# MLP down projections of a two-layer trunk: 24 rows by seven products and 8 plain rows, against all 32 rows by seven products

## Chip, cores and metric

The kernel runs on one core of one Trainium2 chip. The metric is device time in microseconds (us) for one execution of the whole program: both layers, from the input rows to the output rows.

## What is computed

The program is the forward pass of a trunk of two layers over 1024 tokens of width 1024. The part that matters here is the squared-ReLU MLP of each layer, the residual that follows it, and what reads that residual. From the reference, cut:

```python
def squared_relu_mlp(h, w_up, w_down):          # w_up 1024 x 4096, w_down 4096 x 1024
    return jnp.square(jax.nn.relu(h @ w_up)) @ w_down
...
    h = modulate(rmsnorm(x, norm_g[l, 2]), sh_f, sc_f)
    y = squared_relu_mlp(h, mlp_up_w[l], mlp_down_w[l])
    x = x + g_f[:, None, :] * rmsnorm(y, norm_g[l, 3])
```

After layer 0 the next reader of `x` is the attention mixer of layer 1 (`modulate(rmsnorm(x, ...))` times `q_a_w`, and the keys and values). After layer 1 `x` is the output.

## The kernel before

**Numbers.** Each float32 operand is split into a high and a low part (`split_w`, L163 on ACT for the high part, L164 on DVE for the low part), and one product is three matmuls (`mm`, L160): low by high, high by low, high by high. A matmul takes a 128x128 stationary tile and 512 moving columns.

**Seven products.** A down projection is, for a pair of the 128-deep blocks of the 4096 hidden features, a 2 by 2 block product: tokens in two halves of 512, output columns in two halves of 512. `mlp_up` makes the hidden activations, and `sums` (L1052) forms from them seven combined operands, kept in DRAM as `ha0` to `ha6`, one 128x512 tile per pair and operand. `down_pairs` runs through the seven products (Winograd's form of Strassen's seven) as seven **stages**: one operand `ha[which]` against one block of the weights ("11", "12", "21", "22") or a difference of blocks. A stage has its steps over `i`; a step holds two pairs, so four blocks of 128 rows. For each step SP loads a 512 KB operand tile (`raw<-ha`), ACT and DVE split it into a `ring` tile `pa`, the weight block is split into a ring tile `pb`, and PE does 24 matmuls: four token tiles of 128, two blocks, three matmuls. Four PSUM banks (named `one`, or `mm` and `tp`) collect the four token tiles, and at the end of a stage `copy`, `add` or `sums` brings them into the rows `y` (eight tiles of 128 tokens by 1024).

**What the seven products cover.** In the kernel before `ROWS = 8` of the 32 blocks are left out of the pairs: their hidden activations go to DRAM whole (`hd`), and `PAIRS` is 12, six steps per stage. After the seven stages those eight rows are multiplied plainly in `down` (`fill_row` loads and splits a row's weights and activations, 48 matmuls for each of eight token tiles and each group of rows: 384 in all for eight rows, counted in `big<-slot`). The groups are 2, 2 and 4 rows; in the last group each token tile becomes complete in turn.

**The seam.** As a token tile becomes complete, `Seam.tile` adds it to `y` (L300), takes the sum of squares on ACT (L249) and the root (L251, L256), multiplies by the root and the gate on DVE (L306), adds the residual row from DRAM (`xs`, L307), stores the new row and, in layer 0, norms it again for the next layer (`flush`, L289). `Seam.load` brings the residual rows through the same four buffers (`raw_tile`) that all loads use. In layer 0 the normed rows are transposed on PE (L402), scaled and shifted on ACT (L404) and split, and `first_block` multiplies them by the first three column blocks of `q_a_w`, whose three 512 KB loads use the same four buffers. `latent` then takes the norm of those latents; its matmul with `ones` (L1129) is the first that needs a finished latent.

**What sets the order.** The program is written in plain loops, and a scheduler sets the order on each engine from it. `pinned` ties the instructions written inside it to the order in which they are written, on the engines named (all but SP without an argument). Each engine works through its own queue in order. SP issues the loads.

## Time and profile before

| | before |
|---|---|
| runs | 2185.59, 2186.09 and 2193.38 us, median 2186.09 us |
| profiled execution | span 2186.4 us, 0.3 us above the median of the runs |
| instructions | 25316 |
| PE, DVE, ACT busy | 2101.2, 1523.9 and 1052.9 us |
| stages of the program (us from the start) | conv to 397, MLP up of layer 0 to 716, pair stages to 956, plain rows to 1055, latents and attention to 1540, MLP up of layer 1 to 1856, pair stages to 2090, plain rows to 2186.4 |

The profile gives the busy time of each engine, the chain of waits that ended last, groups of equal instructions with their mean time and what ended the idle time ahead of them, and the time of the loads from issue to landing. PE is TensorE's matmuls, DVE is VectorE, ACT is ScalarE, SP issues the loads. Both down projections are short against the whole, so a row must be taken from its stage: the two MLP down projections are the stretches from 716 to 1055 and from 1856 to the end.

### The profile page before, as it was taken

How to read it: one execution, taken by the hardware profiler on the slowest of the kernel's cores; microseconds unless marked ns; L12 is line 12 of the kernel's file. 1: busy time of each engine (PE TensorE's matmuls, PEld its weight loads, DVE VectorE, ACT ScalarE, POOL GpSimd, SP SyncE). 2: the span in 40 equal slices, each digit the busy share in tenths (PEclk: the TensorE clock that was granted, in tenths of full speed). 3: DMA queues.
4: the chain of work that ended last, by engine and by line, in shares of the span. 5: the costliest groups of instructions: out<-in, count | busy, mean ns of one | idle time of the engine just before them, and what ended most of it. 6: DMA issues, size and time to landing. Idle time of an engine off the chain costs nothing.

```text
span 2186.4 us, 25316 instructions
## 1 busy us (share of the span) xinstructions
PE 2101.2 (96%) x9702; PEld 1728.0 (79%) x9702; DVE 1523.9 (70%) x2001; ACT 1052.9 (48%) x1501; POOL 4.0 (0%) x8
## 2 busy tenths in 40 slices
PE   4999999899999999999899999999899999999998
PEld 3778888678888788888777888878688887888886
DVE  6777766876565679776788776665865655566665
ACT  4533354744454444344665555564645444444422
POOL 0000000000000000000000000000000000000000
PEclk9999999999999999999999999999999999999999
DMA  7435464256443985554224231053254544853343
GB/s 226 132 119 152 130 205 139 78 166 194 155 159 117 339 291 189 167 170 143 77 63 125 68 112 44 30 171 128 66 171 155 179 165 149 301 174 97 123 137 116
DMA packets 233551, 323.61 MB, mean 148 GB/s; under 512 B 18165, under 2 KB 141394, under 8 KB 233430
## 3 DMA queue, kind: packets, MB, share of 16 engines
q1 hardware_dynamic: 198424, 244.11, 35.8%
q10 hardware_dynamic: 35006, 77.89, 9.4%
q8 instruction: 76, 1.25, 0.3%
q14 instruction: 45, 0.37, 0.1%
HBM read 244.35 MB, written 77.59 MB: 147 GB/s over the span
## 4 chain that ended last, share of the span: by engine, by line
PE 78%; DVE 12%; ACT 6%; DMA 2%; issue 2%; ACTq 0%; SPq 0%; DVEq 0%
PE one L160 39%; PE mm L160 19%; PE big L160 9%; PE tp L160 6%; ACT junk L249 2%; PE big L1285 2%; DVE y L306 2%; DVE raw L307 2%; PE tp L1311 1%; DVE y L300 1%; DVE acc L190 1%; DVE small L1288 1%; DMA raw<-in_ada_w_dram 1%; DMA aw<-in_ada_w_dram 1%; ACT small L251 1%
## 5 line engine op out<-in xcount | busy, mean ns | idle before, releaser
L160 PE MATMUL one<-slot,uphi 128*128 128x512 f32 x1224 | 378.3, 390 | 0.0
L160 PE MATMUL big<-slot 128*128 128x512 f32 x1536 | 353.0, 390 | 0.5 <-DVE slot L164 0.4
L160 PEld LDWEIGHTS big<-slot 128*128 128x128 f32 x1536 | 287.7, 188 | 60.0 <-DVE slot L164 0.9
L160 PEld LDWEIGHTS one<-slot,uphi 128*128 128x128 f32 x1224 | 230.7, 188 | 48.4 <-issue 0.5
L160 PE MATMUL one<-slot,uplo 128*128 128x512 f32 x612 | 240.9, 394 | 8.1 <-ACT y L568 2.3
L164 DVE TENSOR_TENSOR uplo<-raw,uphi 128x1024 fp32r<-128x1024 f32 x127 | 153.1, 1221 | 133.9 <-ACT uphi L163 133.8
L160 PE MATMUL one<-ring,ring 128*128 128x512 f32 x864 | 197.9, 390 | 3.6 <-DVE ring L164 3.6
L163 ACT ACTIVATE ring<-w 128x1024 fp32r<-128x1024 f32 x84 | 88.9, 1059 | 225.6 <-PE tp L160 117.6
L163 ACT ACTIVATE uphi<-raw 128x1024 fp32r<-128x1024 f32 x127 | 134.5, 1061 | 121.6 <-PE one L160 89.1
L160 PEld LDWEIGHTS one<-ring,ring 128*128 128x128 f32 x864 | 161.7, 188 | 38.7 <-ACT ring L163 3.1
L160 PE MATMUL mm<-slot,uphi 128*128 128x512 f32 x520 | 166.6, 401 | 9.5 <-DVE slot L367 9.3
L164 DVE TENSOR_TENSOR ring<-w,ring 128x1024 fp32r<-128x1024 f32 x84 | 102.7, 1222 | 87.9 <-ACT ring L163 86.1
L160 PEld LDWEIGHTS one<-slot,uplo 128*128 128x128 f32 x612 | 115.5, 189 | 35.4 <-ACT y L493 3.3
L160 PE MATMUL mm<-ring,ring 128*128 128x512 f32 x576 | 139.5, 390 | 0.0
L160 PE MATMUL tp<-ring,ring 128*128 128x512 f32 x576 | 138.7, 389 | 0.0
L190 DVE SCALAR_TENSOR_TENSOR acc<-raw,csil,acc 128x1024 f32<-128x1024 f32 x88 | 112.8, 1282 | 32.3 <-DMA raw<-in_ada_w_dram 30.0
L160 PEld LDWEIGHTS mm<-ring,ring 128*128 128x128 f32 x576 | 107.6, 188 | 23.5 <-issue 0.8
L160 PEld LDWEIGHTS tp<-ring,ring 128*128 128x128 f32 x576 | 108.1, 188 | 22.4
L160 PEld LDWEIGHTS mm<-slot,uphi 128*128 128x128 f32 x520 | 98.9, 192 | 32.8 <-DVE slot L367 10.8
L493 ACT ACTIVATE y<-one 128x512 f32<-128x512 f32 x66 | 39.0, 591 | 163.4 <-PE one L160 102.2
L160 PE MATMUL one<-slot,s 128*128 128x512 f32 x468 | 112.6, 389 | 0.0
L164 DVE TENSOR_TENSOR ring<-raw,ring 128x1024 fp32r<-128x1024 f32 x84 | 102.4, 1219 | 11.8 <-ACT ring L163 11.8
(255 smaller groups left out, 3515.8 us busy)
## 6 DMA issues: line engine op xcount, KB each, us to landing
ha<-y ACTq DMA_DIRECT2D x168, 256.0 KB, 4.2
raw<-ha SPq DMA_DIRECT2D x84, 512.0 KB, 4.1
raw<-in_ada_w_dram SPq DMA_DIRECT2D x80, 512.0 KB, 3.9
raw<-in_mlp_up_w_dram SPq DMA_DIRECT2D x70, 512.0 KB, 4.2
w<-in_mlp_down_w_dram SPq DMA_DIRECT2D x48, 512.0 KB, 6.3
raw<-hd SPq DMA_DIRECT2D x32, 512.0 KB, 4.4
hd<-y ACTq DMA_DIRECT2D x24, 512.0 KB, 3.7
xs<-raw ACTq DMA_DIRECT2D x24, 512.0 KB, 3.0
```

Of the source, the lines that this page charges most:

```text
L160: nc.tensor.matmul(out_, lhs[a], rhs[b], start=first and i == 0, stop=last and i == 2, skip_group_check=more)
L163: nc.scalar.activation(hi, src, AF.Copy)
L164: nc.vector.tensor_tensor(lo, src, hi.bitcast(F32), op=ALU.subtract)
L190: nc.vector.scalar_tensor_tensor(acc, raw, s, acc, op0=ALU.mult, op1=ALU.add)
L249: nc.scalar.activation(junk, src, AF.Square, accum_out=ss)
L251: nc.scalar.activation(rt, ss, AF.Sqrt, bias=eps_d)
L300: nc.vector.tensor_tensor(y, y, p_, op=ALU.add)
L306: nc.vector.scalar_tensor_tensor(y, y, rroot(ss), self.gmb, op0=ALU.mult, op1=ALU.mult)
L307: nc.vector.tensor_tensor(xr, xr, y, op=ALU.add)
L493: nc.scalar.activation(dst, x_, AF.Copy)
L1285: nc.tensor.matmul(o_, a, m_, start=j == 0, stop=j == 4 and b * HALF + w < n)
L1288: nc.vector.tensor_reduce(mx, sp[:, :n], AX.X, ALU.max, negate=True)
```

## The change

All 32 blocks go through the seven products: `PAIRS` is 16, each stage has eight steps, and the plain rows after the stages are gone for the MLP (the groups of plain rows stay for the conv and attention output projections). `hd` keeps only what those two need. `mlp_up` forms the sums for all 16 pairs.

The order of the stages is 0, 1, 3, 6, 4, 5, 2 (by the index of `ha`) as before. Now token half 0 (token tiles 0 to 3) is complete after the fifth stage, and `Seam.tile` runs for these four tiles during the sixth stage, one at every second step; in layer 0 their transposes run during the seventh stage (`seam.front(steps, 2)`). Half 1 (token tiles 4 to 7) is complete at the end of the seventh stage. There the code collects the products of the last `LATE = 4` steps and writes them token tile by token tile, followed by `Seam.tile(4 + t)`. In layer 0 `prep` then loads `q_a_w`, and `first_latents` takes the place of `first_block`: it multiplies half 0 by three column blocks, and the transposes of half 1 are written beside the second of them.

The weight block "21", used in the second and the seventh stage, is no longer kept: both times it is loaded through `raw_tile` (in the seventh stage as the difference 21 - 22, formed in place, L650). There are four `pa` rings and three (from the seventh stage on four) `pb` rings, in place of three and two. Tiles move between pools to make room, and the DMA scratch is set to 256.

```diff
-ROWS = 8
-PAIRS = (D_FF // P - ROWS) // 2
+PAIRS = D_FF // P // 2
+LATE = 4
...
-        def tile(self, t, p_, steps):
+        def tile(self, t, add, steps):
             y = self.ys[t]
-            if t == 0:
-                self.load(0)
-                self.load(1)
-            self.load(t + 2)
+            for i in range(t, t + 3):
+                if i not in self.xr:
+                    self.load(i)
...
+        rings = [ring(r1) for _ in range(7)]
+        pas, pbs = rings[0::2], rings[1::2]
...
                 for i in range(n):
-                    if which in (0, 1, 3, 6):
-                        get(i, b)
+                    wb = ws[b][i] if b != "21" else raw_tile().rearrange("p (q m) -> p q m", q=2)
+                    if which in (0, 1, 3, 6, 2):
+                        get(wb, i, b)
                     if make == "t3":
-                        less(i, "11", "22", "11")
+                        less(wb, ws["22"][i], wb)
                     elif make:
-                        less(i, b, b, make)
+                        less(wb, wb, ws[make][i])
...
+                    if which == 5 and i % 2 == 0:
+                        seam.tile(i // 2, None, [])
+                    if which == 2 and i >= n - LATE:
+                        late.append((pa, pb))
+                        continue
                     for t in range(4):
+                        products(banks_[t], t, pa, pb, i == 0 and not more, i == n - 1, more)
                         if i == n - 1:
                             done(t, banks_[t])
+                    if which == 2:
+                        with pinned():
+                            seam.back()
+                            seam.flush()
+                            seam.front(steps, 2)
...
+            for t in range(4):
+                for j, (pa, pb) in enumerate(late):
+                    products(banks_[t], t, pa, pb, False, j == LATE - 1, True)
+                seam.tile(4 + t, lambda: done(t, banks_[t]), [])
+                if t == 0 and prep:
+                    prep(up)
...
-            if 2 * i < ROWS:
-                for f, t_ in enumerate((a, b)):
-                    nc.scalar.dma_start(hd[2 * i + f], t_)
-            else:
-                late.append(lambda: sums(i - ROWS // 2, *halves(a), *halves(b)))
+            late.append(lambda: sums(i, *halves(a), *halves(b)))
```

Three places of the instruction order follow, before and after. The number behind a name tells tiles apart; that behind `ha` or `xs` is that of one tensor (`ha_109` is `ha[2]`, `ha_112` is `ha[5]`, `xs_104` and `xs_106` are the residual rows of the two layers).

**The loads around the last pair stage of layer 0.** On SP, before, the operand tiles of the seventh stage and the first plain rows:

```order
L115 DMA raw_6797<-ha_109 128x2x512
L115 DMA raw_6828<-ha_109 128x2x512
L115 DMA raw_6859<-ha_109 128x2x512
L115 DMA raw_6865<-in_mlp_down_w_dram 128x1024
L115 DMA raw_6869<-hd_114 128x1024
L115 DMA raw_6898<-ha_109 128x2x512
```

On SP, now, the end of the sixth stage and the start of the seventh:

```order
L115 DMA raw_7059<-xs_104 128x1024
L115 DMA raw_7104<-ha_112 128x2x512
L115 DMA raw_7135<-ha_112 128x2x512
L115 DMA raw_7141<-xs_104 128x1024
L115 DMA raw_7186<-ha_112 128x2x512
L115 DMA raw_7233<-in_mlp_down_w_dram 128x2x512
L115 DMA raw_7236<-ha_109 128x2x512
L115 DMA raw_7285<-in_mlp_down_w_dram 128x2x512
L115 DMA raw_7288<-ha_109 128x2x512
```

Residual rows (`xs`) now stand between the operand tiles, and each step of the seventh stage has two loads, weight and operand, where it had one. `raw_7059` and `raw_7141` are the residual rows of token tiles 4 and 5, whose `Seam.tile` stands after the seventh stage.

On ACT, before, the sixth stage of layer 0 held only the splits of operands and weights:

```order
L163 ACTIVATE ring_5384<-raw_6509 128x1024
L163 ACTIVATE ring_5382<-w_5385 128x1024
L163 ACTIVATE ring_5383<-raw_6546 128x1024
L163 ACTIVATE ring_5380<-w_5386 128x1024
L163 ACTIVATE ring_5381<-raw_6580 128x1024
```

On ACT, now, within the same stage:

```order
L163 ACTIVATE ring_5392<-raw_6971 128x1024
L249 ACTIVATE junk_6900,small_6901<-y_5368 128x1024
L251 ACTIVATE small_6903<-small_6901,eps_d 128x1
L163 ACTIVATE ring_5389<-w_5408 128x1024
L163 ACTIVATE ring_5391<-w_5409 128x1024
L308 DMA xs_105<-raw_6894 128x1024
L249 ACTIVATE junk_6910,small_6911<-raw_6894 128x1024
L163 ACTIVATE ring_5393<-w_5410 128x1024
L251 ACTIVATE small_6913<-small_6911,eps_d 128x1
L249 ACTIVATE junk_6979,small_6980<-y_5369 128x1024
L251 ACTIVATE small_6982<-small_6980,eps_d 128x1
L289 ACTIVATE y_5368<-raw_6894,small_6984 128x1024
```

The last row, the `flush` of token tile 0, is what gives the buffer `raw_6894` back; it now stands behind three splits of weight blocks.

**The seam of layer 0.** On DVE, before, the low parts of `q_a_w` (`uplo`) between the additions of the second group of plain rows (L751):

```order
L164 TENSOR_TENSOR uplo_7233<-raw_7230,uphi_7232 128x1024
L751 TENSOR_TENSOR y_5350<-y_5350,big_7114 128x1024
L164 TENSOR_TENSOR uplo_7239<-raw_7236,uphi_7238 128x1024
L751 TENSOR_TENSOR y_5351<-y_5351,big_7128 128x1024
L164 TENSOR_TENSOR uplo_7245<-raw_7242,uphi_7244 128x1024
L751 TENSOR_TENSOR y_5352<-y_5352,big_7142 128x1024
```

On DVE, now, from the low part of the last operand tile on (L659 is the addition of a finished half row, `y_5372` and `y_5373` are token tiles 4 and 5):

```order
L164 TENSOR_TENSOR ring_5394<-raw_7468,ring_5394 128x1024
L659 TENSOR_TENSOR y_5372<-y_5372,mm_6882 128x512
...
L306 SCALAR_TENSOR_TENSOR y_5372<-y_5372,small_7508,gmb_3771 128x1024
L164 TENSOR_TENSOR uplo_7521<-raw_7518,uphi_7520 128x1024
L307 TENSOR_TENSOR raw_7059<-raw_7059,y_5372 128x1024
L164 TENSOR_TENSOR uplo_7527<-raw_7524,uphi_7526 128x1024
L164 TENSOR_TENSOR uplo_7533<-raw_7530,uphi_7532 128x1024
L659 TENSOR_TENSOR y_5373<-y_5373,mm_6883 128x512
```

The three low parts moved from under the plain rows to between token tiles 4 and 5 of the seam.

**The end of layer 1.** On PE, before, the last plain rows, one token tile after the other:

```order
L160 MATMUL big_16575<-slot_16063 128x512 x3
L160 MATMUL big_16575<-slot_15848 128x512 x3
L160 MATMUL big_16575<-slot_15849 128x512 x3
L160 MATMUL big_16611<-slot_16064 128x512 x3
L160 MATMUL big_16611<-slot_16063 128x512 x3
```

On PE, now, the last steps:

```order
L160 MATMUL mm_16012<-ring_14671,ring_14670 128x512 x6
L160 MATMUL mm_16013<-ring_14671,ring_14670 128x512 x6
L160 MATMUL tp_16014<-ring_14671,ring_14670 128x512 x6
L160 MATMUL tp_16015<-ring_14671,ring_14670 128x512 x6
L160 MATMUL mm_16012<-ring_16325,ring_14672 128x512 x6
L160 MATMUL mm_16013<-ring_16325,ring_14672 128x512 x6
L160 MATMUL tp_16014<-ring_16325,ring_14672 128x512 x6
L160 MATMUL tp_16015<-ring_16325,ring_14672 128x512 x6
```

The products of the last four steps, written token tile by token tile, stand on PE step by step; the four banks of half 1 all receive their last products in the last step. Layer 0 has the same order.

More of the change, by code (lines that the diff above doesn't have):

```diff
@@ L327, in as_quarter @@
         return [(slot[:, kk, :HALF], slot[:, kk, HALF:]) for kk in range(4)]
-    def as_h(slots, pair):
-        return tuple(slots[i].rearrange("p a (b m) -> p (a b) m", b=2) for i in pair)
     def quarter_steps(ys, key, ops):
@@ L672, in sums, with products @@
                 nc.vector.tensor_tensor(spot(half, t, 1), spot(half, t, 1), u, op=ALU.add)
+        def products(p_, t, pa, pb, first, last, more):
+            ts_ = slice(t * P, (t + 1) * P)
+            for q in range(2):
+                mm(p_, (pa[:, 0, q, ts_], pa[:, 1, q, ts_]), (pb[:, 0, q], pb[:, 1, q]), first and q == 0, last and q == 1, more)
         with pinned([mybir.EngineType.SP]):
@@ L731, in down @@
                 slot = slots[f % SLOTS]
-                if f >= 2 or not begun:
-                    fill_row(slot, wd, src_fn, f)
+                fill_row(slot, wd, src_fn, f)
                 rows.append(slot)
@@ L746, in down @@
                 if f == nf:
-                    seam.tile(t, p_, steps)
-                elif f == n_rows and not begun:
+                    seam.tile(t, lambda: nc.vector.tensor_tensor(ys[t], ys[t], p_, op=ALU.add), steps)
+                elif f == n_rows:
                     nc.scalar.activation(ys[t], p_, AF.Copy)
@@ L1006, in trunk_kernel, with down_phase @@
     conv_phase()
-    def down_phase(slots, sizes, wd, src_fn, g, xsrc, xdst, next_w, key, ys=None, pairs=True):
-        begun = ys is not None
-        ys = ys or [row_tile() for _ in range(NT)]
+    def down_phase(slots, sizes, wd, src_fn, g, xsrc, xdst, next_w, key):
+        ys = [row_tile() for _ in range(NT)]
         up = pool("up", "right")
@@ L1442, in trunk_kernel @@
     ys = [row_tile() for _ in range(NT)]
-    ar, slots = down_pairs(ys, mlp_down_w[1], last)
-    banks(False)
-    down(slots, (2, 2, 4), mlp_down_w[1], from_dram(hd), ys, Seam(nx, ys, vtile["g1f"], xs[2], out[0], last=True), [], 0,
-         begun=True)
-    release_arena()
+    down_pairs(ys, mlp_down_w[1], last, Seam(nx, ys, vtile["g1f"], xs[2], out[0], last=True))
     for q in (tp, nx, yp, ad, rawp, cp, wide[0], ps, dr):
```

182 lines of the change are left out of this document (87 added, 95 removed).

## The prediction

> **What bounds the kernel now.** I read the engine totals and the chain of waits first, then the busy time by stage.
>
> ```profile
> PE 2101.2 (96%) x9702; PEld 1728.0 (79%) x9702; DVE 1523.9 (70%) x2001; ACT 1052.9 (48%) x1501; POOL 4.0 (0%) x8
> PE 78%; DVE 12%; ACT 6%; DMA 2%; issue 2%; ACTq 0%; SPq 0%; DVEq 0%
> ```
> ```profile
> 716.00:956.00 240.00, 237.53 (x1076) 196.41 (x1075) 180.58 (x174) 102.24 (x110) 0.00 (x0) 1.00 0.69 234
> 956.00:1055.00 99.00, 95.38 (x430) 78.26 (x429) 74.22 (x84) 45.68 (x73) 0.00 (x0) 0.99 0.47 154
> 1856.00:2090.00 234.00, 232.85 (x1026) 191.86 (x1025) 145.16 (x136) 103.04 (x112) 0.00 (x0) 1.00 0.50 171
> 2090.00:2186.40 96.40, 87.20 (x385) 71.91 (x383) 64.07 (x61) 19.73 (x32) 0.00 (x0) 0.96 0.39 131
> ```
>
> The columns of the second fence are the stretch, its length, then the busy time of PE, weight loads, DVE and ACT. PE is the bound: in the pair stages it is busy 237.53 of 240 and 232.85 of 234 us. Only the two ends of the down projections leave it idle, 3.6 us in the seam and 9.2 us at the end. So removed matmuls are worth their full time, as long as the pair stages stay gapless. Why they are gapless stands in the waits from 716 to 956 and in the chain of PE's work (the last row is a group of DVE operations, with its mean in ns):
>
> ```profile
> ACT ring L163 <- PE tp L160: 59.3, 17, 5.3
> PE one L160 <- DVE ring L164: 2.4, 2, 1.3
> 1926.56 2.72 PE mm L160 x12
> L666 DVE TENSOR_TENSOR y<-y,mm 128x512 f32<-128x512 f32 x4 | 2.8, 688 | 6.1 <-PE mm L160 6.1
> ```
>
> ACT waits for PE to free a ring (59.3 us), not the other way round (2.4 us in all): splits and loads run ahead. Twelve matmuls take 2.72 us, 0.2267 us each, so a step of 24 takes 5.44 us and a stage of eight steps 43.5 us.
>
> **The saving.** Per layer 7 x 12 pairs x 12 matmuls plus 384 for the plain rows make 1392; now 7 x 16 x 12 = 1344. That is 48 fewer, 48 x 0.2267 = 10.9 us per layer and 21.8 us in all. The added sums and stores in MLP up lie under PE (DVE is 70% busy); I cost them at nothing; without that cover they would be 2 layers x 4 pairs x 4 operations of 0.69 us (the half-width DVE operation of the last row), 22 us. The first five stages (217.6 us) keep the run-ahead: their loads, the second stage's weights too, have the four buffers to themselves, and layer 0's ada work on DVE (11 pieces in 8 steps, before 8 in 6) is as dense as before. So I take them gapless but for the first stall of 1.2 us that is there now (1.3 us more, were the one behind it to return).
>
> **The step of the seventh stage.** Here the order decides. Residual rows 4 and 5 sit in two of the four load buffers from the sixth stage to the end of the seventh, since their tiles are finished only then. Two buffers are left for two loads per step, so the next weight can be loaded only when the last one is split. The links of that chain:
>
> ```profile
> raw<-ha SPq DMA_DIRECT2D x19, 512.0 KB, 3.6
> raw<-in_mlp_down_w_dram SPq DMA_DIRECT2D x4, 512.0 KB, 4.2
> w<-in_mlp_down_w_dram SPq DMA_DIRECT2D x21, 512.0 KB, 5.2
> raw<-xs SPq DMA_DIRECT2D x8, 512.0 KB, 3.9
> ```
> ```profile
> L657 DVE TENSOR_TENSOR w<-w,w 128x1024 f32<-128x1024 f32 x24 | 28.8, 1219 | 0.1
> L163 ACT ACTIVATE ring<-w 128x1024 fp32r<-128x1024 f32 x41 | 43.4, 1059 | 116.7 <-PE tp L160 59.3 <-PE one L160 47.0 <-issue 5.2
> L164 DVE TENSOR_TENSOR ring<-raw,ring 128x1024 fp32r<-128x1024 f32 x41 | 50.0, 1218 | 5.3 <-ACT ring L163 5.3
> L289 ACT ACTIVATE y<-raw,small 128x1024 f32<-128x1024 f32 x8 | 9.1, 1142 | 0.2
> ```
>
> The first fence gives issue to landing, the second the mean of one in ns. In quiet stretches a load lands in 3.6 to 4.2 us, under load a weight takes 5.2; two loads are in flight here, and I take 4.0. A link is 4.0 + 1.22 (difference) + 1.06 (high part) + 1.22 (low part) = 7.5 us, against 5.44 us of matmuls: about 2.1 us of PE pause per step. The ends are 7.1 (landing 3.6) and 8.7 (5.2).
>
> **Layer 0, from the first pair product (716.32).** Five stages 217.6, four groups of ada matmuls among them, and the first stall 1.2. A group delays PE by 1.7 us, all by 6.8:
>
> ```profile
> 784.75 1.84 PE L208 MATMUL one<-ones,acc 128*128 128x1 f32 x16
> 786.45 3.03 PE L160 MATMUL mm<-ring,ring 128*128 128x512 f32 x12
> ```
>
> The sixth stage starts at 225.6. In it, the buffer for the operand of step 3 comes back with the flush of tile 0. On ACT that stands behind the split of a weight into a ring that PE frees at the end of the second step, 10.9 us in; then 1.06 + 0.3 + 1.2 + 0.3 + 0.2 + 1.14 us to the end of the flush, 15.1. The load adds 4.0, its split 2.3: 21.4 instead of 16.3, a stall of 5.1. Later steps wait about 2 more for the next buffers: the stage ends at 50.5 rather than 43.5 (bounds 0 and 10 late, were the loads ahead or each step late). The norms of half 0 cost nothing beyond that: on DVE a tile's 1.28 + 1.23 + 0.3 us fall to every second step, beside 2 x 1.22 of splits and the difference where there is one, under 5.44. Half 0's transposes lie in the pauses of the seventh stage. The seventh stage's first weight waits for the split of the sixth's last operand and is ready at 57.0; two links of 6.3 and 7.0 follow (tile 3 gives back a third buffer for one of them) and five of 7.5, so the last weight is ready at 107.8, the last operand 1.2 later, 109.0.
>
> Now the three `q_a_w` loads follow one after another, since each needs the buffer of the one before, and DVE has all three low parts ahead of the addition of tile 5: 3 x (4.2 + 1.06 + 1.22 + 0.2) = 20 us. Tiles 5, 6 and 7 come one after another behind that. The rows of one tile:
>
> ```profile
> 1028.48 1.21 DVE L300 TENSOR_TENSOR y<-y,big 128x1024 f32<-128x1024 f32 x1
> 1034.51 1.22 DVE L300 TENSOR_TENSOR y<-y,big 128x1024 f32<-128x1024 f32 x1
> 1076.48 1.12 PE L1129 MATMUL tp<-sq,ones 128*128 128x512 f32 x2
> ```
>
> The period is 6.03 us with a full-width addition of 1.22; with a half-width one (0.69) 5.5. So tile 7 is added at 109.0 + 20 + 11 = 140, finished 4.9 later, flushed 2.8 after that: 147.7. Only then can half 1 be transposed. On PE 32 transposes (4.2 us) and 45 matmuls (10.2) remain, and 1.9 us to the first matmul with `ones`: 164. Before, it came 1076.48 - 716.32 = 360.2 us after the start; now 225.6 + 164 = 389.6. Layer 0 loses 29.4 us. The ends: without the wait for `q_a_w` 9.4, with landings of 5.2 (eleven links, 1.2 each) 42.6.
>
> **Layer 1.** No flush holds the buffers, the sixth stage loses 1 us. In the seventh, two steps were loaded ahead; the third starts at 56.3, five links later, at 93.8, the last. Then the tail, by the rows of the last tile before:
>
> ```profile
> 2177.24 1.22 DVE L300 TENSOR_TENSOR y<-y,big 128x1024 f32<-128x1024 f32 x1
> 2178.49 1.06 ACT L249 ACTIVATE junk<-y 128x1024 bf16<-128x1024 f32 x1 [3.96 <-DVE y L300]
> 2179.45 0.19 ACT L249 ACTIVATION_READ_ACCUMULATOR junk<-y 128x1 f32 x1
> 2179.67 0.29 ACT L251 ACTIVATE small<-small,eps_d 128x1 f32<-128x1 f32 x1
> 2180.00 0.16 DVE L256 RECIPROCAL small<-small 128x1 f32<-128x1 f32 x1 [1.54 <-ACT small L251]
> 2180.20 1.28 DVE L306 SCALAR_TENSOR_TENSOR y<-y,small,gmb 128x1024 f32<-128x1024 f32 x1
> 2181.51 1.23 DVE L307 TENSOR_TENSOR raw<-raw,y 128x1024 f32<-128x1024 f32 x1
> 2182.77 0.34 ACTq L308 DMA_DIRECT2D out_dram<-raw  x1
> ```
>
> One tile takes 0.7 + 1.2 + 0.3 + 0.2 + 1.3 + 1.2, about 4.9 us, the store another 3.6 to the end of the span. Before, matmuls of 5.44 us per tile covered all but the last tile. Now all four banks receive their last product in the last step, so the four tiles follow one another with next to nothing beneath: 93.8 + 1.4 + 4 x 4.9 + 3.6 = 118.4. With 217.6 + 1.2 the layer takes 337.2 us from its first pair product; before it took 2186.4 - 1859.54, the latter from:
>
> ```profile
> 1859.54 5.60 PE L160 MATMUL one<-ring,ring 128*128 128x512 f32 x24
> ```
>
> That is 326.9, so layer 1 loses 10.3 us (ends: 4 with loads hidden, 17 with landings of 5.2).
>
> **The clock.** Pauses cost more than their length here:
>
> ```profile
> 429.92 0.73 PE L160 MATMUL mm<-slot,uphi 128*128 128x512 f32 x2 [1.42 <-DVE slot L367]
> 430.00:434.00 4.00, 3.39 (x14) 2.47 (x14) 4.00 (x7) 1.69 (x3) 0.00 (x0) 1.00 0.46 133
> 1051.88 1.57 PE L402 MATMUL tp<-cs,y 128*128 128x128 f32 x8 [2.62 <-ACT tt L404]
> 1051.00:1056.00 5.00, 4.11 (x15) 3.29 (x16) 4.49 (x9) 4.38 (x9) 0.00 (x0) 0.68 0.26 105
> 1086.93 0.79 PE L160 MATMUL mm<-slot,uplo 128*128 128x512 f32 x1 [2.02 <-ACT lat L1125]
> 1086.00:1090.00 4.00, 3.07 (x9) 2.57 (x10) 2.42 (x3) 2.93 (x6) 0.00 (x0) 0.62 0.64 169
> ```
>
> After a pause of 1.42 us the granted clock (third number from the end) stays 1.00; after 2.62 and 2.02 it is 0.68 over 5 us and 0.62 over 4, each a loss of about 1.5 us. The pauses of 2.1 us in the seventh stage may close it, but 5.44 + 1.5 is still under 7.5: there it only shortens the pause. It counts after the stall of the sixth stage and ahead of half 1's transposes, 3 us together, and not at all if the gate stays open.
>
> The Trainium skill ("TensorE: Matmul & The Clock Gate", "HAM oscillation — how this bites in real kernels") asks only for no idle gap above about 3.4 us. By that rule the 2.1 us pauses are harmless and only the two long ones count, the same 3 us; the pause of 2.02 us above, followed by 0.62, speaks for the stricter reading.
>
> **Sum.** 29.4 + 10.3 + 3 = 42.7 us on the profiled 2186.4, which is the median of the runs within 0.3: 2229 us, slower by 2%. The saved 21.8 us are within it.
>
> **Rivals.**
> 1. The loads are hidden after all. If buffers come back early enough for loads to run ahead, a step stays 5.44 us. For it speaks today's run-ahead; against it the count of buffers. It decides where landing plus 3.5 us drops below 5.44, a landing of 1.9, and the quietest row has 3.6. Layer 0 would then have its last split at 86, and with 20 + 11 + 7.7 + 16.3 lose 6.4; layer 1 would gain 2: 2191. With the `q_a_w` loads overlapping as well (13 less) 2178. This is the case that ends not slower.
> 2. Contention: operand, weight and residual loads land in 5.2 us as the weights do under load: (11 + 5) x 1.2 = 19 more, 2248. Against it, the seventh stage moves only 1 MB per 7.5 us.
> 3. Only layer 0 loses: layer 1's run-ahead carries it through its seventh stage, so that it keeps a gain of 2 instead of a loss of 10.3, and the sixth stage's stall is absorbed (7 + 1.5): 2208.
> 4. The clock stays low through both seventh stages. Twice 0.2267 is 0.453 us per matmul, 10.9 us a step, 3.4 over the link: 12 steps make 41, 2270. Against it, a PE that is slower than its loads has no pauses left.
>
> **Chances.** The forecast 0.57, within 2212 to 2247; the first rival 0.17, a third of it below 2175; the second 0.12; the third 0.10; the fourth 0.04. A measurement of this kernel can tell a change from none from about 0.5%, 11 us. Faster by more than that 0.05, within it 0.12, slower 0.83. The range from 2198 to 2252 leaves out the first rival and the fourth.
>
> **What would show it.** In the trace after: PE pauses of about 2 us at each step of the seventh stages, ended by a DVE split, and the weight loads (`raw<-in_mlp_down`) issued one link apart; a PE stall near 5 us at the fourth step of layer 0's sixth stage; some 30 us with little PE work ahead of half 1's transposes, its DVE rows `uplo` waiting for `q_a_w`; four tile chains of 4.9 us one after another at the end. It is wrong if the seventh stages are gapless, or if the pair stages before them stall.

## The result, and the profile after

The changed kernel takes 2246.15 us (median of four runs, 2244.79 to 2249.75), the kernel before beside it 2186.53 us: a ratio of 1.027, with a 95% interval of 1.026 to 1.028. The forecast was 2229 us, within 2198 to 2252. The profiled execution has a span of 2247.9 us, 61.5 us more than before (the medians differ by 59.6), at a mean granted clock of 0.978 (before 0.991); the granted clock is the share of TensorE's full clock that the profile records.

The page's engine totals and chain of waits after:

```profile
PE 2095.7 (93%) x9606; PEld 1717.3 (76%) x9606; DVE 1531.4 (68%) x2017; ACT 1085.5 (48%) x1533; POOL 4.0 (0%) x8
PE 72%; DVE 13%; ACT 7%; DMA 6%; issue 2%; ACTq 0%; SPq 0%; DVEq 0%
```

The 96 matmuls are gone (9702 to 9606), but PE's part of the chain fell from 78% to 72%, and that of DMA rose from 2% to 6%: transfers have come onto the path. Busy time by stretch (start and end, length, PE, weight loads, DVE, ACT, POOL, granted clock, DMA share, GB/s); the first four stretches are the first five pair stages, the sixth, the seventh and the seam of layer 0; the last four cover the pair stages of layer 1 and its tail, without regard to the stages, of which the sixth starts at 2126.05 and the seventh at 2172.38:

```profile
715.85:942.43 226.58, 225.43 (x1025) 187.17 (x1024) 166.64 (x156) 97.30 (x105) 0.00 (x0) 1.00 0.73 250
942.43:1001.49 59.06, 47.20 (x194) 37.80 (x192) 35.33 (x43) 27.31 (x40) 0.00 (x0) 0.93 0.40 134
1001.49:1058.60 57.11, 51.47 (x224) 41.00 (x224) 32.52 (x33) 27.72 (x34) 0.00 (x0) 0.95 0.46 147
1058.60:1112.30 53.70, 26.31 (x114) 20.31 (x114) 25.39 (x38) 25.85 (x41) 0.00 (x0) 0.71 0.27 88
1906.85:2133.40 226.55, 225.40 (x994) 186.13 (x993) 138.33 (x127) 100.32 (x111) 0.00 (x0) 1.00 0.51 177
2133.40:2178.80 45.40, 42.62 (x186) 34.28 (x184) 30.71 (x31) 15.90 (x19) 0.00 (x0) 1.00 0.52 181
2178.80:2228.60 49.80, 41.25 (x167) 32.05 (x167) 24.02 (x22) 13.68 (x15) 0.00 (x0) 0.97 0.47 147
2228.60:2247.90 19.30, 0.03 (x1) 0.00 (x0) 10.78 (x13) 4.33 (x9) 0.00 (x0) 0.60 0.27 109
```

The first five stages of layer 0 are as gapless as before (225.43 of 226.58 us). Its sixth and seventh stage take 59.1 and 57.1 us, where eight gapless steps would take 43.5, the seam has PE busy for half of its time, and layer 1 ends with 19.3 us without matmuls. PE's rows in the sixth and seventh stage of layer 0 (start, duration; in brackets the idle time ahead and what ended it):

```profile
963.30 5.49 PE L160 MATMUL mm<-ring,ring 128*128 128x512 f32 x12 [4.39 <-DVE ring L164]
...
1001.49 5.49 PE L160 MATMUL mm<-ring,ring 128*128 128x512 f32 x12 [6.48 <-DVE ring L164]
...
1038.32 3.02 PE L160 MATMUL mm<-ring,ring 128*128 128x512 f32 x12 [1.55 <-DVE ring L164]
...
1045.57 3.02 PE L160 MATMUL mm<-ring,ring 128*128 128x512 f32 x12 [1.51 <-DVE ring L164]
...
1052.85 3.04 PE L160 MATMUL mm<-ring,ring 128*128 128x512 f32 x12 [1.54 <-DVE ring L164]
```

The last steps start 7.25 and 7.28 us apart. One link of that period, from SP's and DVE's rows:

```profile
1037.16 0.37 SPq L115 DMA_DIRECT2D raw<-in_mlp_down_w_dram  x1
1040.80 1.23 DVE L650 TENSOR_TENSOR raw<-raw,w 128x1024 f32<-128x1024 f32 x1 [2.53 <-DMA raw<-in_mlp_down_w_dram]
1043.15 2.36 DVE L164 TENSOR_TENSOR ring<-raw,ring 128x1024 fp32r<-128x1024 f32 x2 [1.13 <-ACT ring L163]
1044.41 0.37 SPq L115 DMA_DIRECT2D raw<-in_mlp_down_w_dram  x1
```

The weight is issued at 1037.16, its difference formed 3.6 us later, its high part made (the 1.13 us in which DVE waits for ACT), its low part is done at about 1044.4, and only then the next weight is issued: 7.25 us, and no link of this chain overlaps another. Behind the last step, DVE's low parts of `q_a_w`, the addition of token tile 5 and PE's next transposes:

```profile
1066.03 1.23 DVE L164 TENSOR_TENSOR uplo<-raw,uphi 128x1024 fp32r<-128x1024 f32 x1 [5.08 <-ACT uphi L163]
1072.45 1.23 DVE L164 TENSOR_TENSOR uplo<-raw,uphi 128x1024 fp32r<-128x1024 f32 x1 [5.19 <-ACT uphi L163]
1073.59 0.68 DVE L659 TENSOR_TENSOR y<-y,mm 128x512 f32<-128x512 f32 x1
```
```profile
1079.30 0.45 PE L399 MATMUL tp<-cs,y 128*128 128x128 f32 x1 [11.03 <-DVE y L659]
1112.30 1.10 PE L1139 MATMUL tp<-sq,ones 128*128 128x512 f32 x2
```

And the end of layer 1, where the four tiles follow one another 4.9 us apart:

```profile
2229.48 0.68 DVE L659 TENSOR_TENSOR y<-y,mm 128x512 f32<-128x512 f32 x1
2234.36 0.68 DVE L659 TENSOR_TENSOR y<-y,tp 128x512 f32<-128x512 f32 x1
2239.25 0.68 DVE L659 TENSOR_TENSOR y<-y,tp 128x512 f32<-128x512 f32 x1
2244.24 0.34 ACTq L308 DMA_DIRECT2D out_dram<-raw  x1
```

The 61.5 us by place, all read from PE's rows in the two profiled executions: the down projection of layer 0 (first pair product to the first matmul with `ones`) 360.2 to 396.5, that of layer 1 326.9 to 341.1; from that `ones` matmul to the first matmul of the attention output projection 360.9 to 370.4; MLP up (from the transposes at 395.60 and 392.25 in layer 0, at 1538.78 and 1582.85 in layer 1, to the first pair product) 320.7 to 323.6 and 320.8 to 324.0; the conv part 3.4 shorter and the output projection 1.3 shorter. The first two places are those of the forecast (+50.5 us); the others (+11) it did not have.

### The profile page after: what moved, and what is told of

The parts are those of the page before. It is cut to its first block, busy times and chain, and to the rows that moved or that the text cites. A ratio compares the mean times of both kernels' runs of the same rounds, so it can differ in the third digit from the quotient of the medians.

```text
span 2247.9 us, 25315 instructions
## 1 busy us (share of the span) xinstructions
PE 2095.7 (93%) x9606; PEld 1717.3 (76%) x9606; DVE 1531.4 (68%) x2017; ACT 1085.5 (48%) x1533; POOL 4.0 (0%) x8
## 4 chain that ended last, share of the span: by engine, by line
PE 72%; DVE 13%; ACT 7%; DMA 6%; issue 2%; ACTq 0%; SPq 0%; DVEq 0%
PE one L160 40%; PE mm L160 18%; PE tp L160 5%; PE big L160 4%; PE big L1294 2%; DMA raw<-in_mlp_down_w_dram 2%; ACT junk L249 2%; DVE y L306 1%; DVE ring L164 1%; DVE raw L307 1%; ACT ring L163 1%; PE tp L1320 1%; DMA raw<-ha 1%; DVE acc L190 1%; DVE small L1297 1%
## 5 line engine op out<-in xcount | busy, mean ns | idle before, releaser
L160 PE MATMUL one<-ring,ring 128*128 128x512 f32 x1152 | 263.3, 390 | 2.3 <-DVE ring L164 2.3
L160 PEld LDWEIGHTS one<-ring,ring 128*128 128x128 f32 x1152 | 215.8, 188 | 48.4 <-ACT ring L163 3.1
L163 ACT ACTIVATE ring<-raw 128x1024 fp32r<-128x1024 f32 x144 | 149.4, 1053 | 189.8 <-DMA raw<-ha 98.4
L164 DVE TENSOR_TENSOR ring<-raw,ring 128x1024 fp32r<-128x1024 f32 x144 | 174.1, 1221 | 91.7 <-ACT ring L163 91.6
L160 PE MATMUL mm<-ring,ring 128*128 128x512 f32 x768 | 193.9, 403 | 28.8 <-DVE ring L164 28.8
L160 PEld LDWEIGHTS mm<-ring,ring 128*128 128x128 f32 x768 | 147.1, 194 | 65.8 <-DVE ring L164 35.1
L160 PE MATMUL tp<-ring,ring 128*128 128x512 f32 x768 | 185.1, 390 | 0.0
L160 PE MATMUL big<-slot 128*128 128x512 f32 x768 | 179.7, 395 | 4.8 <-DVE slot L164 4.5
L160 PEld LDWEIGHTS big<-slot 128*128 128x128 f32 x768 | 145.4, 190 | 36.0 <-DVE slot L164 5.2
L160 PE MATMUL mm<-slot,uphi 128*128 128x512 f32 x344 | 108.4, 397 | 9.5 <-DVE slot L364 9.3
```

The source lines that it names most:

```text
L160: nc.tensor.matmul(out_, lhs[a], rhs[b], start=first and i == 0, stop=last and i == 2, skip_group_check=more)
L163: nc.scalar.activation(hi, src, AF.Copy)
L164: nc.vector.tensor_tensor(lo, src, hi.bitcast(F32), op=ALU.subtract)
```

## The experiments

The theory: the residual rows of tiles 4 and 5 hold two of the four load buffers through the seventh stage, so each step waits for its load; tails and the `q_a_w` loads then stand exposed. A join below is the place where a phase's first matmuls wait for what the phase ahead of it leaves. Rivals: the order of the late products on PE, contention of the transfers, and, for the places that the forecast lacked, the memory of the slots and the added sums. The stretches of all the runs that are compared, in us of their profiled executions:

| | start to first pair product | layer 0, to `ones` | to attention output | to pair product of layer 1 | layer 1, to the end | median of the runs |
|---|---|---|---|---|---|---|
| before | 716.3 | 360.2 | 360.9 | 422.2 | 326.9 | 2186.5 |
| changed | 715.9 | 396.5 | 370.4 | 424.1 | 341.1 | 2246.15 |
| x1 rows late | 714.6 | 367.6 | 370.3 | 422.7 | 318.2 | 2196.1 |
| x2 products pinned | 716.4 | 395.0 | 369.5 | 422.9 | 345.2 | 2253.1 |
| x3 `q_a_w` last | 715.7 | 389.0 | 369.0 | 423.1 | 341.8 | 2239.0 |
| x5 rows late, by step | 716.0 | 372.8 | 368.0 | 424.0 | 328.1 | 2210.1 |
| x6 five buffers | 730.9 | 366.1 | 368.5 | 434.2 | 319.6 | 2223.7 |
| x7 `q_a_w` in the stage | 718.5 | 357.0 | 369.6 | 423.8 | 317.9 | 2186.8 |
| x9 join | 715.8 | 358.4 | 364.4 | 429.9 | 318.3 | 2188.7 |
| x12 best | 714.6 | 354.9 | 364.7 | 423.2 | 316.2 | 2177.5 |

**x1: residual rows of tiles 4 and 5 loaded only after stage 6.**

```diff
-                if i not in self.xr:
+                if i not in self.xr and (t >= 4 or i < 4 or add):
```

> The changed kernel, but the residual rows of token tiles 4 and 5 are loaded after the seventh stage and not during the sixth, so that all four load buffers serve the seventh stage. Buffer theory: the links of 7.2 us (1031.04, 1038.32, 1045.57 in layer 0's trace) fall to 5.44 us plus the transposes; layer 0's seventh stage then ends about 17 us earlier (6.5 at its start, 1.5 at each of its later steps), layer 1's about 11 us earlier (the eight pauses of its last eleven steps, 0.45 to 2.40, add up to 11.3); the seams behind them move along. 28 us less than the changed kernel, about 2218. Rival (the step is set by the splits on DVE and ACT, or by the speed of the loads, whatever the buffers): links stay at 7.2, 2246.

Measured 2196.1 us (ratio to before 1.003, 1.002 to 1.005), 50 us less than the changed kernel and not 28. From the start of the sixth stage to the last pair product the two layers got 16.3 and 12.3 us shorter (116.2 to 99.9 and 102.6 to 90.3), which are the 28 expected. The rest lies behind the stages: the scheduler, by itself, now put the late products token tile by token tile on PE, so the tails of three tiles went under matmuls too. PE's largest group of late-stage matmuls, in the changed kernel and in x1 (count, busy time, mean ns, idle time ahead):

```profile
L160 PE MATMUL mm<-ring,ring 128*128 128x512 f32 x768 | 193.9, 403 | 28.8 <-DVE ring L164 28.8
```
```profile
L160 PE MATMUL mm<-ring,ring 128*128 128x512 f32 x768 | 187.6, 395 | 8.3 <-DVE ring L164 6.6
```

28.8 us of waiting for splits become 8.3 us of waiting, 6.6 of them for splits. But two things changed at once, so the next two separate them.

**x2: the buffers as in the changed kernel, the late products pinned on PE token tile by token tile.**

```diff
+                with pinned([mybir.EngineType.PE]):
                     for j, (pa, pb) in enumerate(late):
                         products(...)
```

> The changed kernel, but the products of the last four steps stay on PE in the order in which they are written, token tile by token tile. Buffer theory: the last step's splits come as late as before, the first token tile needs them, and the three others (16.3 us) come behind; each tile's norm of 4.9 us then lies under 5.44 us of matmuls. From the last split to the end of layer 1: 1.4 + 16.3 + 4.9 + 3.6 = 26.2 us against 1.4 + 4 x 4.9 + 3.6 = 24.6 now: no gain, 0 to 4 us more in all, 2246 to 2250. Rival (the order of the products is what costs): the four norms are covered, layer 1 gains about 12 us, layer 0 as much, 2222 to 2234.

Measured 2253.1 us, 7.0 more than the changed kernel and 3 above what was expected, 1.030 of before (1.028 to 1.032). With the loads 7.3 us apart PE has only the first token tile's six of a step's 24 matmuls between two waits, and the pauses grow from 1.5 us to 4.3 to 5.6 us; two of them in layer 1:

```profile
2205.16 2.93 PE L160 MATMUL mm<-ring,ring 128*128 128x512 f32 x6 [5.42 <-DVE ring L164]
2212.61 2.93 PE L160 MATMUL mm<-ring,ring 128*128 128x512 f32 x6 [4.52 <-DVE ring L164]
```

Order alone wins nothing while the buffers are held.

**x5: the buffers free as in x1, the late products pinned step by step as the changed kernel had them.**

```diff
-            for t in range(4):
-                for j, (pa, pb) in enumerate(late):
-                    products(...)
+            with pinned([mybir.EngineType.PE]):
+                for j, (pa, pb) in enumerate(late):
+                    for t in range(4):
+                        products(...)
```

> Residual rows of the tiles from 4 on are loaded only after stage 6, as in the first run, and the products of the last six pairs stand step by step on PE in both layers, as in the changed kernel. It separates the two things that the first run changed together: the buffers that the rows hold, and the order of the late products. Buffers as the cause of the gaps at each step: no pause before the steps of the seventh stage; in layer 1 the four tiles' tails stand exposed (from PE's end four tile periods of 4.9 us and 3.6 us, about 19 us instead of the 8.8 us of the first run), in layer 0 the chain of the token half 1 norms sets the end as in the first run (0 to 2 us more): 2202 to 2210 us. Order as the cause: the gaps come back, 2240 to 2250 us. Tails that cost nothing: 2196 us.

Measured 2210.1 us (1.011, 1.009 to 1.013), the upper end of 2202 to 2210. The pauses of the seventh stage are gone with the order unchanged; layer 1 is 9.9 us longer than x1 (328.1 against 318.2), which is the exposed tails. In layer 0 it costs 5.2 us, more than the 0 to 2 expected: with all four banks finished in the last step, half 1's transposes start behind a longer pause.

```profile
1056.06 0.45 PE L399 MATMUL tp<-cs,y 128*128 128x128 f32 x1 [8.86 <-DVE y L659]
```

So of the 50.0 us between the changed kernel and x1, 36 belong to the buffers and 14 to the order that free buffers let the scheduler choose. The two don't simply add: with the buffers held, the same order cost 7 us (x2).

**x6: five load buffers, rows loaded early as in the changed kernel.**

```diff
-... name=nm("raw"), bufs=4)
+... name=nm("raw"), bufs=5)
```

> Five load buffers instead of four; residual rows loaded in stage 6 as in the changed kernel (the late products then come out token tile by token tile on PE). With two buffers held by the residual rows, three are left for the two loads of a step. Buffers as the cause: a load is always under way while a step is split, the steps of the seventh stage stand without pauses and the sixth stage's pause (5.49 us in the changed kernel) shrinks too: pair start to first ones-matmul of layer 0 about 357 to 368 us, layer 1 about 318 us, sum 2186 to 2198 us. Contention of the rows' transfers, not the buffers: pauses stay at about 1.5 us a step and the time stays at 2235 to 2246 us.

Measured 2223.7 us (1.017, 1.015 to 1.019), against 2186 to 2198 expected. In the stages in dispute it did what the buffers' theory says: 366.1 and 319.6 us (expected 357 to 368, and 318), with the rows' transfers as in the changed kernel. The pauses of layer 0's sixth and seventh stage are at most 0.9 us, those of layer 1's two of 1.6 and 1.5, so contention falls. (The pause that the expectation puts at 5.49 us is 4.39; 5.49 is the time of the matmuls behind it.) The rest of the forecast missed because PE now waits 7.4 us ahead of the first pair product in both layers, among other pauses outside the stages:

```profile
730.87 39.49 PE L160 MATMUL one<-ring,ring 128*128 128x512 f32 x163 [7.44 <-DVE ring L164]
```

Why a fifth buffer brings the first operand late there was not pursued.

**x3: `q_a_w` loaded after tile 7 instead of between tiles 4 and 5.**

```diff
-                if t == 0 and prep:
+                if t == 3 and prep:
```

> The changed kernel, but the three loads of the query down weights are written after token tile 7 and not after tile 4. Theory (they hold tiles 5 to 7 on DVE): the pauses of 11.03, 3.15, 5.55 and 4.52 us ahead of half 1's transposes shrink; tiles 5 to 7 follow tile 4 at 5.5 us each, the last flush comes 14 us earlier, about 2232. Rival (the norms' own chain sets it, the loads only lie beside it): less than 3 us, 2243 to 2246. A third way: the loads, now later, hold the first latents instead, so that only part of the 14 us is kept, 2236 to 2240.

Measured 2239.0 us, 7.2 less. The seam got shorter by 7.5 us and not by the whole chain of 20, since the first latents now wait in its place:

```profile
1070.39 0.76 PE L160 MATMUL big<-h,uplo 128*128 128x512 f32 x1 [11.80 <-DVE small L256]
```

**x7: as x1, with `q_a_w` loaded and split at the start of the late steps of the seventh stage.**

```diff
+                    if which == 2 and i == n - LATE and prep:
+                        prep(up)
...
-                if t == 0 and prep:
-                    prep(up)
```

> As the first run (residual rows of the tiles from 4 on loaded after stage 6), and the query down-projection operands for the next attention loaded and split at the start of the seventh stage's late steps instead of between tiles 4 and 5. If what is left in layer 0 (367.6 us from the pair start to the first ones-matmul, against 360.2 in the kernel before) is the chain of the query operands that holds tile 5 on DVE: 8 to 12 us less than the first run, 2184 to 2188 us. If the splits instead delay the late steps on the ring: pauses in the seventh stage of layer 0 by as much as they win, 2194 to 2200 us.

Measured 2186.8 us (1.000, 0.999 to 1.001), inside 2184 to 2188. Layer 0's down projection gets 10.6 us shorter than in x1 (357.0 after 367.6) and is now shorter than before the change (360.2). The splits hardly delay the stage: it has pauses of 0.58 and 1.73 us, and x1 had one of 1.66.

**x4: the first slots of the attention output projection in other memory.**

```diff
-        return pools, s[1] + s[0]
+        return pools, s[0] + s[1]
```

> The changed kernel, but the first weight slots of the output projections are taken from the right-hand pool and not from the left. The trace of the change lost 8 us where the attention output projection starts (its first matmul stands behind a pause of 4.54 us, its first split comes only after the attention's last tile; before, the splits began four tiles earlier). Theory (the first slots lie on memory that the attention's working tiles hold to their end): the splits begin earlier, 5 to 9 us less, 2237 to 2241. Rival (the splits wait for ACT and DVE, which are busy with the attention): 2246.

Measured 2253.2 us (1.030). The pause ahead of the output projection stayed 4.54 us, with ACT's splits where they were, and a new pause of 4.31 us ahead of the conv output projection brought the first pair product 4.8 us later: other memory for the slots does not move the splits. The rows of the changed kernel show what PE waits for: ACT makes the first slot only behind the last attention output.

```profile
1478.21 0.60 ACT L1355 ACTIVATE o<-mm 128x512 f32<-128x512 f32 x1 [1.05 <-PE mm L160]
1478.83 0.33 ACTq L1356 DMA_DIRECT2D hd<-o  x1
1479.21 3.90 ACT L163 ACTIVATE slot<-raw 128x1024 fp32r<-128x1024 f32 x4 [0.40 <-ACT o L1355]
```
```profile
1482.71 7.51 PE L160 MATMUL big<-slot 128*128 128x512 f32 x20 [4.54 <-DVE slot L164]
```

In the kernel before the same splits stood amid the attention's last tiles, two of them at:

```profile
1433.87 2.00 ACT L163 ACTIVATE slot<-raw 128x1024 fp32r<-128x1024 f32 x2
```

**x9: as x7, the first two rows of that projection filled ahead of the last attention output, their order pinned on ACT; the first three slots come from the right-hand pool, opened ahead of these outputs.**

```diff
-    before.turn(2)
-    before.mul()
-    before.turn()
-    before.mul(2)
+    pp.release()
+    ara = pool("arA", "right")
+    slots = slots_of(ara, 3)
+    with pinned([mybir.EngineType.Activation]):
+        before.turn(2)
+        fill_row(slots[0], attn_o_w[0], from_dram(hd), 0)
+        before.mul()
+        before.turn()
+        fill_row(slots[1], attn_o_w[0], from_dram(hd), 1)
+        before.mul(2)
...
+    slots = slots + slots_of(ar[1], 3)
```

> As x7_qa_in_stage (2186.77 us), and the first two rows of the attention output projection are loaded and split by ACT ahead of the last attention output, not behind it. In the changed kernel PE waits 4.54 us there and the stretch from the first ones-matmul to that projection's first matmul is 370.4 us, against 360.9 us in the kernel before; in x7 it is 369.6 us. If ACT's order there is the cause: 5 to 9 us less than x7, 2178 to 2182 us. If the rows' loads or the memory of their slots is what is late: 2186 us.

Measured 2188.7 us (1.001, 1.000 to 1.002): no gain, where 2178 to 2182 were expected. The join did get 5.2 us shorter (364.4 after 369.6). The first slots lie on the same side as in x4, which kept its pause, so it is the order that x9 adds. But 6 us came back at the next join:

```profile
1438.55 0.73 PE L160 MATMUL big<-slot 128*128 128x512 f32 x2 [0.79 <-DVE slot L164]
```
```profile
1868.42 21.95 PE L160 MATMUL one<-ring,ring 128*128 128x512 f32 x86 [6.22 <-DVE ring L164]
```

**x8: the changed kernel without the sums of the first four pairs.**

```diff
+            if i < 4:
+                for j, t_ in enumerate((a0, a1, b1, b0, a0, a1, b0)):
+                    nc.scalar.dma_start(ha[j][i], t_)
+                return
```

> The changed kernel without the combined operands of the first four pairs (part of the computation is left out: the raw gated values are stored in place of their sums, so that bytes and transfers stay the same). The sums were costed at nothing in the prediction; MLP up took 2.9 and 3.2 us longer in the two layers. If DVE's additions ahead of the next pair's work make that: 3 to 6 us less, 2240 to 2243 us. If it is the larger stores or something else: 2246 us.

Measured 2251.3 us, 2246.3 to 2252.1, against the changed kernel's 2244.8 to 2249.8: no gain. MLP up of layer 0 (391.28 to 716.21) took 324.9 us, no less than the 323.6 with the sums. DVE's additions alone are not what lengthens it.

**x10 and x11: as x9, with the stores of those pairs on SP (x10) or GpSimd (x11) instead of ACT.**

```diff
-                nc.scalar.dma_start(ha[j][i], t_)
+                (nc.sync if i < 4 else nc.scalar).dma_start(ha[j][i], t_)
```

> As x9_join, and the stores of the combined operands of the first four pairs are issued by SP instead of ACT. Without their sums MLP up was as slow as with them (x8), so the sums' time on DVE is not the cause; on ACT the split of the next pair's weights stands behind the issue of the stores, which wait for the last sum (5.62 us for five of them in the changed kernel). If that queue is the cause: 3 us less per layer, 4 to 6 us less than x9 in all, MLP up from the last conv transposes to the first pair product back at 320.7 us. If SP's stores hold the loads behind them instead: no gain or 1 to 5 us more.

> As x10, with the same stores issued by GpSimd, which has next to nothing else in its queue. If ACT's queue is the cause: 4 to 6 us less than x9. If both x10 and x11 stand at x9's time, the cause of the slower MLP up is the bytes of the stores or something else, not the queue that issues them.

Measured 2190.7 us (1.001, 1.000 to 1.002) and 2219.3 us (1.016, 1.014 to 1.018). On SP MLP up of layer 0 is 322.4 us, with x9's 322.7; on GpSimd it is 339.3, with single waits of PE for splits and results of up to 7.0 us. ACT's queue alone is not the cause either. What the trace shows of the 3 us stands in the next section.

**x12: as x9, with the slots four and two on the two sides of the memory and the late operands of MLP up on the sides as in x7, and two residual rows instead of three loaded at the start of the sixth stage.**

```diff
-            for i in range(t, t + 3):
+            for i in range(t, t + (3 if add else 2)):
...
-        hs = {n: as_quarter(slots[i]) for n, i in zip(names, (2, 3, 0, 1, 4, 5))}
+        hs = {n: as_quarter(slots[i]) for n, i in zip(names, (2, 3, 4, 5, 0, 1) if done else (2, 3, 0, 1, 4, 5))}
...
-    slots = slots + slots_of(ar[1], 3)
+    slots = slots + slots_of(ar[3], 1) + slots_of(ar[1], 2)
```

> As x9_join, with two edits. (1) In x9 the join got shorter (364.4 us from the first ones-matmul to the projection's first matmul, 369.6 in x7) but the first product of layer 1's pair stages then waited 6.22 us for a low part; the operand slots lay three and three on the two sides of the memory there. Now they lie four and two as in x7, so the late operands of MLP up stand in memory that the rings don't take. If that is the cause: the pause ahead of the first pair product of layer 1 is gone, 5 to 6 us less than x9. (2) Tile 0 of the sixth stage loads two residual rows instead of three, so one more buffer is left for the operand of step 3: the pause of 4.39 us at that step (in x7 at 965.89 us) shrinks below 2 us, 3 to 5 us less. Together 2177 to 2183 us, against 2188.7 (x9) and 2187.0 (the kernel before). If the slots' place is not the cause, the 6.22 us stay; if the operand of step 3 waits for something else than a buffer, the 4.39 us stay.

Measured 2177.5 us (0.996 of before, 0.994 to 0.997), inside 2177 to 2183 and faster than both kernels. The 6.2 us ahead of layer 1's pair products are gone (423.2 after 429.9), and so is the pause at the sixth stage's step 3; the longest idle time left in layer 0's stages is 1.9 us. Its engine totals and the group of late-stage matmuls:

```profile
PE 2077.1 (96%) x9606; PEld 1705.3 (78%) x9606; DVE 1528.0 (70%) x2017; ACT 1082.9 (50%) x1533; POOL 4.0 (0%) x8
```
```profile
L160 PE MATMUL mm<-ring,ring 128*128 128x512 f32 x768 | 186.2, 391 | 4.0 <-DVE ring L164 4.0
```

PE is busy 24.1 us less than before the change, about the 21.8 us that the 96 matmuls are worth; the time falls by 10.3 us.

## Why the prediction was right, point by point

The forecast held 42.7 of the 61.5 us; of the 18.8 us that it lacked, 7.8 lie in the places that it named and 11 in places that it did not. In the places that it named the mechanism is the one that was forecast. The 11 nearly carried the total out of 2212 to 2247: nothing in the forecast stood for them, and that they were not larger is luck.

- **The saving** (21.8 us, if the stages stay gapless) is real but was eaten: the down projections of the two layers lost what the forecast gave as 39.7 us and its 3 us for the clock; measured together 36.3 + 14.2 = 50.5 us.
- **The step of the seventh stage** (7.5 us; ends 7.1 and 8.7) measured 7.1 to 7.3 us over the last five links of layer 0, with the landing nearer to 3.6 than to the 4.0 taken. In layer 1 the steps start 6.9 to 7.4 us apart, and once 8.1. x1, x5 and x6 show that the held buffers make it.
- **The sixth stage of layer 0**: forecast a stall of 5.1 at step 3 and the next stage's first weight ready at 57.0, its operand 1.2 later; measured 4.39 us at 963.30, and the next stage starts at 59.1. The stall was the buffer that was named: the load of that step's operand follows the end of the flush of tile 0 at once, in the rows below 14.8 us after the stage's start (forecast 15.1), and x12 removed the stall by leaving one row unloaded. The seventh stage's first step waited for its operand and not for its weight: the operand's load was issued at 995.53, only when the weight had been split.

```profile
956.03 1.14 ACT L289 ACTIVATE y<-raw,small 128x1024 f32<-128x1024 f32 x1
957.20 0.36 SPq L115 DMA_DIRECT2D raw<-ha  x1
```

- **The chain to `ones`**: last operand split 109.0 after the sixth stage's start, measured 110.4 (the low parts from 1050.44 end at 1052.8), partly by errors that cancel: the seventh stage starts 0.9 us late, its first two steps take 15.3 us and not 13.3, the five links behind them 36.1 and not 37.5; the `q_a_w` chain 20, measured 20.8 (1052.8 to 1073.59); the rest 35, measured 38.7 (1073.59 to 1112.30), with the granted clock at 0.71 over the seam. In sum 164 against 169.9. x3 showed that not all of the 20 us can be had by moving the loads behind the tiles, x7 that 10.6 can by moving them ahead.
- **Layer 1**: seventh stage's last split 93.8 after the sixth stage's start, measured 96.8 (2126.05 to 2222.89); from there 24.6 to the end, measured 25.0. In sum 10.3 against 14.2; the tails themselves were right to half a microsecond.
- **The clock** (3 us): pauses of 2 us were taken to close the gate or not, and the traces show both. Here the pauses of 1.5 us in layer 0's seventh stage left twelve matmuls at 3.0 us, and so did 1.83 us in layer 1; behind 2.40 us twelve took 4.61, behind 4.39 and 6.48 us 5.49. The rows below, two of the changed kernel, one of x2 and two of x3, show that near 2 us the length of the gap alone does not decide: 1.84 and 1.92 us lowered the clock, 2.05 us did not. What else decides is not shown. The Trainium skill ("TensorE: Matmul & The Clock Gate", "HAM oscillation — how this bites in real kernels") asks for no idle gap above about 3.4 us; the traces disagree, with 4.37 us for twelve matmuls behind a gap of 1.84.

```profile
2186.18 3.06 PE L160 MATMUL mm<-ring,ring 128*128 128x512 f32 x12 [1.83 <-DVE ring L164]
...
2201.54 4.61 PE L160 MATMUL mm<-ring,ring 128*128 128x512 f32 x12 [2.40 <-DVE ring L164]
```
```profile
2183.09 4.61 PE L160 MATMUL mm<-ring,ring 128*128 128x512 f32 x12 [1.92 <-DVE ring L164]
```
```profile
2191.27 3.01 PE L160 MATMUL mm<-ring,ring 128*128 128x512 f32 x12 [2.05 <-DVE ring L164]
...
2213.58 4.37 PE L160 MATMUL mm<-ring,ring 128*128 128x512 f32 x12 [1.84 <-DVE ring L164]
```

- **What was costed at nothing and was not**: the added sums and stores in MLP up, 6 us in both layers (the bound given was 22). Of the 2.9 us in layer 0, 1.3 are PE's waits, the largest a new one of 1.13 us for DVE at 465.4. About 1 us is the clock: in the rows below (first before, then now; the third number from the end is the clock) PE works for 3.41 and for 5.50 us at half speed, and of the 2.1 us more half are lost. Why that spell doubled is open, and neither the sums of the first four pairs (x8) nor ACT's store queue (x10) alone accounts for the rest.

```profile
438.42:441.83 3.41, 3.41 (x9) 2.63 (x10) 2.71 (x5) 0.63 (x1) 0.00 (x0) 0.50 0.45 116
```
```profile
433.62:440.45 6.83, 5.50 (x13) 4.34 (x14) 5.63 (x10) 2.32 (x3) 0.00 (x0) 0.50 0.49 159
```

- **What was not in the forecast**: the join with the attention output projection, 9.5 us, where the scheduler now puts ACT's first slot splits behind the last attention output. x9 won 5.2 us there by fixing that order, so the order is the larger part; the rest, and why the scheduler chose it, is open. The forecast costed only the stretches that the change was written in.
- **The rivals**: loads hidden (2191) did not happen, but x1 made that case by freeing the buffers and came out at 2196.1. Contention (2248) gives nearly the measured time, but by the wrong mechanism: it takes landings of 5.2 us, the weight's difference starts 3.6 us after its issue, and x6 with the same transfers has none of layer 0's pauses above 0.9 us. Layer 0 alone, and a clock low throughout, are excluded by layer 1's +14.2 us and the 3.0 us per twelve matmuls.

## What to carry to other kernels

Count the buffers that a moved step holds, and for how long: a load issued early for a late reader takes a buffer from every load in between, and here two of four made a chain of load, difference and two splits out of what had run ahead. Fewer matmuls are worth their time only if the loads still lead; taking the early loads back turned +60 us into +9, moving the seam's weights into the stage into 0, and fixing the order at the attention output projection together with the sixth stage's buffer into -10. When a scheduler sets the order, look at the joins far from the edit as well: 9.5 of the 61.5 us came from one.

## What the runs showed of the hardware

TensorE's granted clock fell behind some idle gaps of 1.84 us (x3) and 1.92 us (x2), with twelve matmuls at 4.37 and 4.61 us instead of 3.0, and not behind others of 1.83 us and 2.05 us (changed kernel, x3). In the changed kernel, behind 4.39 and 6.48 us, twelve took 5.49 us. Where it fell in the traces of all these runs it fell to 0.50, and for 3.4 us or a whole multiple of that, but for the last spell, which the program's end cuts off. The stores of the combined operands of four pairs, issued by GpSimd, made MLP up of layer 0 339.3 us long; issued by SP 322.4, by ACT 322.7.
